# One transformer-like step on one core: slabs of gate_f on GpSimd's queue, an earlier split of a raw tile, and squares of the residual added by VectorE

## Chip, cores and metric

The kernel runs on one core of one Trainium2 chip. The metric is device time in microseconds (us) of one execution, as the median of the runs. Engines are named as in the profile: PE is TensorE (PEld its weight loads), DVE is VectorE, ACT is ScalarE, POOL is GpSimd, SP is SyncE. SP only issues DMAs here; ACT and POOL issue some too. L309 and the like are line numbers of the kernel before.

## What is computed

One layer over 128 context tokens and 256 latent tokens, 384 in all, with a model width of 2048. The part that the change touches is the second half, the MLP:

```python
def _layer(x, mod, ...):
    shift_a, scale_a, gate_a, shift_f, scale_f, gate_f = [mod[:, i][:, None, :] for i in range(N_MOD)]
    ...
    x = x + gate_a * _rmsnorm(mix, norm_w[1])
    h = _rmsnorm(x, norm_w[2]) * (1 + scale_f) + shift_f
    y = jnp.square(jax.nn.relu(h @ w1)) @ w2          # w1: 2048 x 8192, w2: 8192 x 2048
    x = x + gate_f * _rmsnorm(y, norm_w[3])
    return x, C, n, m
```

`mod` is `silu(cond) @ ada_w + ada_b` with ada_w of 2048 x 12288; the condition is one vector for the context tokens and one for the latent tokens. Everything is float32.

## The kernel before

**Products in three parts.** A float32 product is made of three faster ones: each operand is split into `hi` (a copy rounded to fp32r, made by ACT, L138 or L1223) and `lo = raw - hi` (made by DVE, L139 or L1224), and TensorE adds hi*hi, hi*lo and lo*hi (mm3, or `product` in mlp_seven). Every weight tile is 128 x 1024 floats and thus costs one load, one ACT pass and one DVE pass. Four `hi` and four `lo` buffers stand between the splitting engines and TensorE (N_W), so both can run about four tiles ahead.

**The order of work.** In the MLP a planner lays out each engine's instructions: it takes them in the order in which the code asks for them, but an instruction that is ready by its own reckoning may go ahead of one asked for earlier that is not. Once laid out, each engine and each DMA queue runs strictly in order. A `Feed` steps a side generator along a main loop: `first_side` is stepped once after each weight tile of the first w1 groups.

**The stage of the first w1 groups (some 615 to 670 us).** `make_h2` turns each of 16 tiles of the residual into the hi and lo parts of the MLP's input h2, with five DVE passes and two ACT passes that matter (L1025 to L1033). `gemm_T` over the first three w1 groups asks for h2 tiles 0 to 3 with its first weight tile, 4 to 7 with its fourth, 8 to 11 with its seventh and 12 to 15 with its tenth. Beside it `first_side` asks for the squares of the same 16 tiles: ACT squares a tile (L1046), and POOL (tiles 1 to 11) or DVE (tiles 12 to 15) adds it into `sqb` (L1047). The sum goes through TensorE (L925) to the factor `r2bc`, which the evaluation of the w1 groups needs.

**Chunks 1 to 6 of the MLP (some 810 to 1560 us).** A chunk is eight tiles of the hidden width. For each there are four groups of w1 (`w1_group`, four weight tiles each) and two blocks of w2 (`mlp_seven`, one for each half of the output). A block works on a 2 x 2 scheme with seven products: raw tiles b11, b21, b22 and b12 are loaded (L1218) and split, then differences of raw tiles are made by DVE in place (L1271, L1280, L1288, L1300) and split too, 14 splits in all. A chunk 7 with one such block closes the MLP.

**gate_f.** The last of the six modulation vectors is made on the side, by DVE: `ada_vec` loads a slab of ada_w (L309), multiplies it by the condition and adds it into an accumulator (L324, L326), once for each of the two conditions. Its first parts run in the earlier stages. Its last two parts run in chunks 1 to 4: 16 slabs of 128 x 512 floats each, through one buffer (`slab=512, bufs=1`, L1347), so that a slab's load waits for the DVE steps on the slab before it. Their loads stand on SP's queue among the loads of w1 (L132) and w2 (L1218). POOL's queue has the stores of x1 (L1055) until 740 us and the loads of x1 and gate_f for the end of the kernel from 1552 us on (L1149, L1155).

Of the kernel before, what the change touches and what calls it, by code (L numbers as in the profile page):

```python
# [10 lines left out]
ALU = mybir.AluOpType  # L11
# [5 lines left out]
NTOK = 384  # L17
# [11 lines left out]
N_ADA = 4  # L29
# [15 lines left out]
def hymba_kernel(  # L45
# [6 lines left out]
    nc = tc.nc  # L52
# [6 lines left out]
    adap = ada_scope.enter_context(tc.tile_pool(name="adap", bufs=1, side="right"))  # L59
# [239 lines left out]
    vec = {}  # L299

    def ada_vec(i, c, n):


        acc = vec["acc"].tile([P, 2, n], F32, tag="adaacc", name=f"ada_acc_{i}_{c}", bufs=1)
        c0, nj = i * D + c, vec["slab"] // n

        def load(t):
            raw = vec["pool"].tile([P, nj, n], F32, tag="ada", name=f"ada_raw_{i}_{c}_{t}", bufs=vec["bufs"])
            nc.sync.dma_start(raw, aw[:, nj * t:nj * t + nj, c0:c0 + n])  # L309
            return raw  # L310

        beside = vec.get("beside", {})
        raw = load(0)
        yield
        for t in range(16 // nj):
            if t in beside:
                next(beside[t], None)
            more = t < 16 // nj - 1
            ahead = load(t + 1) if more and vec["bufs"] > 1 else None
            for a in range(nj):  # L320
                for g in range(2):
                    cj = sg[:, g, nj * t + a:nj * t + a + 1]
                    if t == 0 and a == 0:
                        nc.vector.tensor_scalar(acc[:, g, :], raw[:, a, :], cj, None, op0=ALU.mult)  # L324
                    else:
                        nc.vector.scalar_tensor_tensor(acc[:, g, :], raw[:, a, :], cj, acc[:, g, :], op0=ALU.mult, op1=ALU.add)  # L326
            raw = load(t + 1) if more and ahead is None else ahead
            if more:
                yield
        yield  # L330
        w = n // 2
        nk = w // P
        if "end" in beside:
            next(beside["end"], None)
        ps = bank(f"adav_{i}_{c}")
        for h in range(2):
            for g in range(2):
                r = 32 * (2 * h + g)
                nc.tensor.matmul(ps[r:r + 32, 0:w], ones[:, 0:32], acc[:, g, h * w:(h + 1) * w], start=True, stop=True)
        sb = vec["pool"].tile([P, 512], F32, tag="adasb", name=f"adav_sb_{i}_{c}", bufs=1)  # L340
        nc.scalar.activation(sb[:, 0:w], ps[:, 0:w], AF.Copy)
        yield
        pf = bank(f"adaf_{i}_{c}")
        for k in range(nk):
            nc.tensor.matmul(pf[:, 4 * k:4 + 4 * k], sb[:, k * P:(k + 1) * P], ident[:, 0:P:32], start=True, stop=True)
        for h in range(2):
            ada_finish(i, c // P + nk * h, nk, pf[:, 0:4 * nk].rearrange("p (k r) -> p k r", r=4)[:, :, 2 * h:2 * h + 2])
        yield
# [87 lines left out]
    h = []  # L436
# [389 lines left out]
    att_scope = ExitStack()  # L826
    acc_scope = ExitStack()
    accp = acc_scope.enter_context(tc.tile_pool(name="accp", bufs=1, side="right", reuse_waits="tile"))
    vec.update(pool=adap, acc=accp, slab=1024, bufs=N_ADA)
    att = att_scope.enter_context(tc.tile_pool(name="att", bufs=2, reuse_waits="tile"))  # L830

    gslab = att.tile([P, 1, 512], F32, name="gslab", bufs=1)
# [205 lines left out]
            make_h2(len(h2))  # L1038
        return h2[k]

    def square_x1(k, eng):
        if k == 0:
            nc.scalar.activation(sqb[:, 0:NTOK], mo[k][:, 0:NTOK], AF.Square)
            return
        t = slot(f"sq_x1{k}")
        nc.scalar.activation(t[:, 0:NTOK], mo[k][:, 0:NTOK], AF.Square)  # L1046
        eng.tensor_tensor(sqb[:, 0:NTOK], sqb[:, 0:NTOK], t[:, 0:NTOK], op=ALU.add)  # L1047

    def store_x1():
        for k in range(KT):  # L1050
# [59 lines left out]
    late = []  # L1110

    def first_side():
        for n in range(3):
            if n == 0:
                with tc.issue_after(mm3.ins):
                    next(gfg)
            yield
            for k in range(4 * n, 4 * n + 4):
                square_x1(k, nc.gpsimd)
            yield  # L1120
            yield
        for k in range(12, 16):
            square_x1(k, nc.vector)
        yield
        late.append(nc.vector.tensor_copy(r2bc, token_rstd_rows([sqb], "r2")[:, 0:NTOK]).ins)
        yield
        yield
        yield from store_x1()
# [80 lines left out]
    def mlp_seven(ch, q, r16, r7):  # L1209
# [50 lines left out]
        for h in range(2):  # L1260
            b11, b21 = raws[0, 0, h], raws[1, 0, h]
            w = split(b21, f"b21{h}")
            product("yz0", 1, 0, h, w)
            product("2", 1, 1, h, w)
            if h == 0:
                w = split(raws[0, 0, 1], "b111")
                for js in ((0,), (1,)):
                    product("x", 0, 0, 1, w, js=js)
                    product("1", 0, 1, 1, w, js=js)
            b22, b12 = raws[1, 1, h], raws[0, 1, h]  # L1270
            tt(b11, b12, b11, op=ALU.subtract)  # L1271
            w = split(b22, f"b22{h}")
            product("yz1", 1, 0, h, w, stop=False)
            product("3", 2, 2, h, w)
            if h == 0:
                yx = ys[0].rearrange("p (a q) -> p a q", a=2)
                tt(yx, banks["x"].unsqueeze(1).to_broadcast([P, 2, 512]), yx, op=ALU.add)
            else:
                add(ys[0][:, 0:512], "yz0")
            tt(b12, b22, b12, op=ALU.subtract)  # L1280
            w = split(b11, f"t1{h}")
            product("yz1", 0, 0, h, w, start=False)
            product("4", 2, 0, h, w)
            if h == 0:
                keep(r16[:, q, 0], "1")
            else:
                add(ys[1][:, 0:512], "2")
            tt(b22, b22, b11, op=ALU.subtract)  # L1288
            free.append(b11)
            if h == 0:  # L1290
                load(1, 1, 1)
            w = split(b12, f"t3{h}")
            product("7", 0, 2, h, w)
            free.append(b12)
            if h == 0:
                load(0, 1, 1)
            else:
                add(ys[1][:, 512:], "3")
                add(ys[0][:, 512:], "yz1")
            tt(b21, b21, b22, op=ALU.subtract)  # L1300
            w = split(b22, f"t2{h}")
            product("6", 2, 1, h, w)
            free.append(b22)
            if h == 1:
                add(ys[2][:, 512:], "4")
                keep(r7[:, q], "7")
            w = split(b21, f"t4{h}")
            product("5", 1, 2, h, w)
            free.append(b21)
# [21 lines left out]
    for ch in range(8):  # L1331
# [6 lines left out]
        elif ch <= S_LAST:  # L1338
            if ch == S_FIRST:
# [4 lines left out]
                    scope.close()  # L1344
                str_scope = ExitStack()
                strp = str_scope.enter_context(tc.tile_pool(name="strp", bufs=1, side="right", reuse_waits="tile"))
                vec.update(pool=strp, acc=strp, slab=512, bufs=1, half=False)  # L1347
                ff.rate = RATE_GS
                r16, r7 = strp.tile([P, 2, 2, 512], F32, name="r16"), strp.tile([P, 2, 512], F32, name="r7")
                for n in range(3):  # L1350
# [80 lines left out]
```

## Time and profile before

| | us |
|---|---|
| median of 3 runs | 1679.78 |
| lowest and highest | 1679.76, 1680.25 |
| the profiled execution | 1679.09 |
| its span (first instruction to last) | 1677.4 |
| granted TensorE clock, mean | 0.998 |

In the views of the profile, "a <- b" in a list of waits means that a waited for b; a row of the timeline has its start from the span's beginning, its length, engine, line, operation, output and inputs, and in brackets the idle time of the engine before it. A run of equal instructions on one engine is one row with its count, and its length is that of the whole run. Where an engine has work all the time but shares of it wait for nothing, its speed alone counts: TensorE is in that state for nearly the whole MLP, so that a wait of another engine matters only where it makes TensorE wait.

### The profile page before, as it was taken

What the parts mean: (1) busy time and instruction counts of PE and PEld (TensorE: products, weight loads), DVE (VectorE), ACT (ScalarE), POOL (GpSimd) and SP (SyncE); (2) the same over time, 40 slices, a digit from 0 to 9 for tenths busy, and PEclk for the clock granted to TensorE, in tenths of its full rate; (3) what the DMA queues carried; (4) which work ended last, traced back from release to release, by engine and by line L of the source; (5) the groups of instructions that cost most, each with busy time, mean ns of one, the idle gap of its engine ahead of it and who ended that gap; (6) DMA issues with size and microseconds to landing.
All of it is one profiled execution on the core that took longest, in us unless ns stands there. A gap on an engine that the chain in (4) does not pass through costs nothing.

```text
span 1677.4 us, 24412 instructions
## 1 busy us (share of the span) xinstructions
PE 1648.3 (98%) x9249; PEld 1496.6 (89%) x9249; DVE 1328.4 (79%) x1971; ACT 751.1 (45%) x1224; POOL 133.1 (8%) x185
## 2 busy tenths in 40 slices
PE   6999999999999999999999999999999999999997
PEld 4888999999999989989988988988988988988986
DVE  3677669898999959997688787589788488488687
ACT  5322345555443345543444444444445354354452
POOL 1000002221000024530000000000000000000220
PEclk9999999999999999999999999999999999999999
DMA  9999757787789964754446445255544343443662
GB/s 328 329 309 304 246 175 247 239 250 229 239 262 309 319 202 137 213 153 126 136 150 203 125 133 177 87 169 162 153 151 136 116 151 116 136 125 112 197 193 103
DMA packets 231461, 320.72 MB, mean 191 GB/s; under 512 B 14784, under 2 KB 169872, under 8 KB 230960
## 3 DMA queue, kind: packets, MB, share of 16 engines
q1 hardware_dynamic: 223920, 303.42, 57.3%
q0 software_dynamic: 5984, 13.78, 2.9%
q10 hardware_dynamic: 1440, 1.97, 0.3%
q8 instruction: 72, 1.18, 0.3%
q14 instruction: 45, 0.37, 0.1%
HBM read 308.61 MB, written 10.51 MB: 190 GB/s over the span
## 4 chain that ended last, share of the span: by engine, by line
PE 78%; DVE 13%; DMA 5%; issue 3%; ACT 0%; POOL 0%; SPq 0%; DVEq 0%; ACTq 0%; POOLq 0%
PE acc_w L151 10%; PE acc_w L150 10%; PE acc_w L149 10%; PE v L512 4%; PE u L512 4%; PE y L1239 3%; PE y L1240 3%; PE y L1238 3%; DVE ada_acc L326 3%; DMA ada_raw<-in_ada_w_dram 2%; DVE lo_t L1224 2%; PE y L1082 2%; PE y L1083 2%; PE y L1081 2%; PE y_yz L1240 1%
## 5 line engine op out<-in xcount | busy, mean ns | idle before, releaser
L150 PE MATMUL acc_w<-h2l,hi_w 128*128 128x384 f32 (+1 forms) x1024 | 346.0, 338 | 0.5 <-DVE h2l L1033 0.5
L149 PE MATMUL acc_w<-h2h,hi_w 128*128 128x384 f32 (+1 forms) x1024 | 344.7, 338 | 1.2 <-ACT h2h L1029 1.2
L151 PE MATMUL acc_w<-h2h,lo_w 128*128 128x384 f32 (+1 forms) x1024 | 344.9, 337 | 0.6 <-DVE lo_w L139 0.6
L326 DVE SCALAR_TENSOR_TENSOR ada_acc<-ada_raw,sg,ada_acc 128x1024 f32<-128x1024 f32 (+1 forms) x240 | 252.8, 1081 | 32.1 <-DMA ada_raw<-in_ada_w_dram 32.1
L149 PEld LDWEIGHTS acc_w<-h2h,hi_w 128*128 128x128 f32 x1024 | 192.2, 188 | 4.0 <-ACT h2h L1029 2.0
L150 PEld LDWEIGHTS acc_w<-h2l,hi_w 128*128 128x128 f32 x1024 | 192.5, 188 | 1.8 <-DVE h2l L1033 0.8
L151 PEld LDWEIGHTS acc_w<-h2h,lo_w 128*128 128x128 f32 x1024 | 192.1, 188 | 2.2 <-DVE lo_w L139 1.9
L139 DVE TENSOR_TENSOR lo_w<-raw_b,hi_w 128x1024 fp32r<-128x1024 f32 x52 | 62.9, 1219 | 37.5 <-ACT hi_w L138 37.5
L139 DVE TENSOR_TENSOR lo_w<-raw_a,hi_w 128x1024 fp32r<-128x1024 f32 x52 | 63.1, 1219 | 35.7 <-ACT hi_w L138 35.6
L138 ACT ACTIVATE hi_w<-raw_b 128x1024 fp32r<-128x1024 f32 x52 | 54.9, 1057 | 62.7 <-PE acc_w L150 47.6
L138 ACT ACTIVATE hi_w<-raw_w 128x1024 fp32r<-128x1024 f32 x48 | 50.7, 1055 | 68.7 <-PE acc_w L150 36.5
L1223 ACT ACTIVATE hi_t<-raw_b 128x1024 fp32r<-128x1024 f32 x52 | 55.2, 1062 | 58.5 <-PE y L1240 28.3
L1223 ACT ACTIVATE hi_t<-raw_a 128x1024 fp32r<-128x1024 f32 x52 | 55.2, 1061 | 54.3 <-PE y L1240 26.5
L138 ACT ACTIVATE hi_w<-raw_a 128x1024 fp32r<-128x1024 f32 x52 | 54.8, 1057 | 53.6 <-PE acc_w L150 41.0
L139 DVE TENSOR_TENSOR lo_w<-raw_w,hi_w 128x1024 fp32r<-128x1024 f32 x48 | 58.4, 1218 | 22.0 <-ACT hi_w L138 21.9
L138 ACT ACTIVATE hi_wo<-raw_wo 128x1024 fp32r<-128x1024 f32 x32 | 33.9, 1063 | 80.1 <-DMA raw_wo<-in_w_out_dram 65.1
L1224 DVE TENSOR_TENSOR lo_b<-raw_b,hi_b 128x1024 fp32r<-128x1024 f32 x40 | 48.8, 1221 | 24.9 <-ACT hi_b L1223 24.6
L1223 ACT ACTIVATE hi_b<-raw_a 128x1024 fp32r<-128x1024 f32 x38 | 40.2, 1058 | 62.2 <-PE acc_w L150 46.2
L1223 ACT ACTIVATE hi_b<-raw_b 128x1024 fp32r<-128x1024 f32 x40 | 42.3, 1057 | 56.6 <-PE acc_w L150 45.3
L1224 DVE TENSOR_TENSOR lo_b<-raw_a,hi_b 128x1024 fp32r<-128x1024 f32 x38 | 46.2, 1221 | 22.4 <-ACT hi_b L1223 22.4
L1224 DVE TENSOR_TENSOR lo_t<-raw_a,hi_t 128x1024 fp32r<-128x1024 f32 x52 | 63.0, 1214 | 0.3 <-ACT hi_t L1223 0.2
L1224 DVE TENSOR_TENSOR lo_t<-raw_b,hi_t 128x1024 fp32r<-128x1024 f32 x52 | 62.9, 1215 | 0.0
(2286 smaller groups left out, 4243.7 us busy)
## 6 DMA issues: line engine op xcount, KB each, us to landing
ada_raw<-in_ada_w_dram SPq DMA_DIRECT2D x130, 512.0 KB, 5.2
raw_a<-in_w_dram SPq DMA_DIRECT2D x104, 512.0 KB, 4.1
raw_b<-in_w_dram SPq DMA_DIRECT2D x104, 512.0 KB, 4.2
raw_w<-in_w_dram SPq DMA_DIRECT2D x48, 512.0 KB, 4.2
raw_wo<-in_w_out_dram SPq DMA_DIRECT2D x32, 512.0 KB, 5.3
u<-in_ada_w_dram SPq DMA_DIRECT2D x18, 512.0 KB, 5.9
raw_u<-in_w_in_dram SPq DMA_DIRECT2D x16, 512.0 KB, 7.0
raw_q<-in_w_in_dram SPq DMA_DIRECT2D x16, 512.0 KB, 5.0
```

The source lines that it names most:

```text
L138: nc.scalar.activation(hi[:, 0:n], raw[:, 0:n], AF.Copy)
L139: low = lambda: nc.vector.tensor_tensor(lo[:, 0:n], raw[:, 0:n], hi[:, 0:n].bitcast(F32), op=ALU.subtract)
L149: nc.tensor.matmul(ps, lh, rh, start=start, stop=False)
L150: nc.tensor.matmul(ps, lh, rl, start=False, stop=False)
L151: mm3.ins = nc.tensor.matmul(ps, ll, rh, start=False, stop=stop).ins
L326: nc.vector.scalar_tensor_tensor(acc[:, g, :], raw[:, a, :], cj, acc[:, g, :], op0=ALU.mult, op1=ALU.add)
L512: nc.tensor.matmul(acc[i][:, 0:n], h[k0 + k][a][:, i * P:(i + 1) * P], (hi, lo)[b][:, k, :], start=k == 0 and a + b == 0, stop=k == nk - 1 ...
L1223: nc.scalar.activation(hi, raw, AF.Copy)
L1224: nc.vector.tensor_tensor(lo, raw, hi.bitcast(F32), op=ALU.subtract)
L1238: nc.tensor.matmul(banks[m], xh, wh, start=start and h + j == 0, stop=False)
L1239: nc.tensor.matmul(banks[m], xh, wl, start=False, stop=False)
L1240: nc.tensor.matmul(banks[m], xl, wh, start=False, stop=stop and h + j == 2)
```

## The change

Three edits that have nothing to do with each other.

1. The queue of `ada_vec`'s loads is given by its caller: SP's for the parts before chunk 1, POOL's for the last two parts of gate_f (32 slabs of 256 KB).
2. In a block of mlp_seven the split of b22 is asked for before, not after, the difference `b12 - b11`. Both were there before; neither reads what the other writes.
3. All adds of the squares are on DVE. `first_side` asks for squares 0 to 3 in its fourth step (before: second), 4 to 7 in its seventh (before: fifth), 8 to 15 in its tenth (before: 8 to 11 in the eighth, 12 to 15 in the tenth). The step that makes r2bc is the eleventh, as before.

```diff
@@ ada_vec
-            nc.sync.dma_start(raw, aw[:, nj * t:nj * t + nj, c0:c0 + n])
+            vec["queue"].dma_start(raw, aw[:, nj * t:nj * t + nj, c0:c0 + n])
...
-    vec.update(pool=adap, acc=accp, slab=1024, bufs=N_ADA)
+    vec.update(pool=adap, acc=accp, slab=1024, bufs=N_ADA, queue=nc.sync)
...
-    def square_x1(k, eng):
+    def square_x1(k):
...
-        eng.tensor_tensor(sqb[:, 0:NTOK], sqb[:, 0:NTOK], t[:, 0:NTOK], op=ALU.add)
+        nc.vector.tensor_tensor(sqb[:, 0:NTOK], sqb[:, 0:NTOK], t[:, 0:NTOK], op=ALU.add)
...
     def first_side():
+        with tc.issue_after(mm3.ins):
+            next(gfg)
         for n in range(3):
-            if n == 0:
-                with tc.issue_after(mm3.ins):
-                    next(gfg)
-            yield
-            for k in range(4 * n, 4 * n + 4):
-                square_x1(k, nc.gpsimd)
             yield
             yield
-        for k in range(12, 16):
-            square_x1(k, nc.vector)
+            yield
+            for k in range(4 * n, 4 * n + 4 if n < 2 else 16):
+                square_x1(k)
         yield
...
@@ mlp_seven
             b22, b12 = raws[1, 1, h], raws[0, 1, h]
+            w = split(b22, f"b22{h}")
             tt(b11, b12, b11, op=ALU.subtract)
-            w = split(b22, f"b22{h}")
             product("yz1", 1, 0, h, w, stop=False)
...
-                vec.update(pool=strp, acc=strp, slab=512, bufs=1, half=False)
+                vec.update(pool=strp, acc=strp, slab=512, bufs=1, half=False, queue=nc.gpsimd)
```

## What I predicted

> **What bounds the kernel now.** I read the page's busy times and its chain first, then TensorE's waits, then the table of windows, and only then the lines that the change touches.
>
> ```profile
> PE 1648.3 (98%) x9249; PEld 1496.6 (89%) x9249; DVE 1328.4 (79%) x1971; ACT 751.1 (45%) x1224; POOL 133.1 (8%) x185
> PE 78%; DVE 13%; DMA 5%; issue 3%; ACT 0%; POOL 0%; SPq 0%; DVEq 0%; ACTq 0%; POOLq 0%
> ```
>
> TensorE is busy for 98% of the span and holds 78% of the chain. All three edits act on other engines, so they can move the end only where TensorE waits for those. The waits of TensorE by releaser, first from 618 to 640 us (the first w1 groups, where the squares lie), then from 640 us to the end (total, times, longest):
>
> ```profile
> PE acc_w L149 <- ACT h2h L1029: 0.6, 1, 0.6
> PE acc_w L150 <- DVE h2l L1033: 0.5, 1, 0.5
> ...
> PE y L1238 <- ACT hi_t L1223: 1.4, 1, 1.4
> PE acc_w L151 <- DVE lo_w L139: 0.6, 2, 0.3
> PE y L1239 <- DVE lo_t L1224: 0.3, 1, 0.3
> PE y L1082 <- DVE lo_w L139: 0.2, 1, 0.2
> PE y_yz L1239 <- DVE lo_b L1224: 0.2, 1, 0.2
> ```
>
> That is 1.1 us and 2.7 us. What all three edits can save while TensorE has work is thus some 4 us, or 0.23% of the run. What they can cost has no such cap.
>
> Does time that TensorE gains at 636 us reach the end? It does if VectorE waits for TensorE further on. The table of windows (length, then busy time of PE, PEld, DVE, ACT, POOL; granted clock; DMA share; GB/s):
>
> ```profile
> 780.00:820.00 40.00, 40.00 (x236) 39.34 (x235) 19.76 (x31) 16.03 (x25) 0.00 (x0) 1.00 0.49 151
> 908.00:945.00 37.00, 37.00 (x213) 37.00 (x212) 23.21 (x35) 14.12 (x22) 0.00 (x0) 1.00 0.66 198
> 945.00:987.00 42.00, 42.00 (x199) 36.16 (x198) 39.58 (x47) 21.92 (x27) 0.00 (x0) 1.00 0.41 122
> 1208.00:1247.00 39.00, 39.00 (x182) 33.27 (x181) 37.75 (x45) 20.20 (x24) 0.00 (x0) 1.00 0.40 116
> ```
>
> From 780 to 820 us VectorE is busy for 19.76 of 40 us beside a full TensorE: it follows TensorE, and an earlier TensorE carries it along. The second row is a stretch of w1 groups: 213 matmuls in 37.0 us, 0.174 us each. In the blocks of mlp_seven (the last two rows) it is nearly full, 39.58 of 42 us and 37.75 of 39 us. There its lead is spent, and there the waits of 2.7 us lie.
>
> **The squares (square_x1, first_side).** Removed from GpSimd are 11 adds, added to VectorE are 11. GpSimd's adds together (min/median/max in ns), the last of the four that VectorE has already, GpSimd's first three, VectorE's and ScalarE's rows beside them, and TensorE's two waits:
>
> ```profile
> L1047 POOL TENSOR_TENSOR sqb<-sqb,sq_x x11: 1003/1222/3058, 624.0 to 652.8; 128x384 f32<-128x384 f32 x11
> 661.96 0.55 DVE L1047 TENSOR_TENSOR sqb<-sqb,sq_x 128x384 f32<-128x384 f32 x1
> 623.98 3.41 POOL L1047 TENSOR_TENSOR sqb<-sqb,sq_x 128x384 f32<-128x384 f32 x3 [11.14 <-ACT sq_x L1046]
> 601.28 0.24 DVE L297 TENSOR_TENSOR mod<-mod,prmT 128x8 f32<-128x8 f32 x2
> 624.53 0.69 DVE L297 TENSOR_TENSOR mod<-mod,prmT 128x4 f32<-128x4 f32 x1
> 625.40 0.91 DVE L297 TENSOR_TENSOR mod<-mod,prmT 128x4 f32<-128x4 f32 x1
> 626.62 1.31 DVE L1030 SCALAR_TENSOR_TENSOR h2l<-mo,mod,h2h 128x128 fp32r<-128x128 f32 x2
> 634.40 0.74 DVE L1030 SCALAR_TENSOR_TENSOR h2l<-mo,mod,h2h 128x128 fp32r<-128x128 f32 x2
> 634.08 1.75 ACT L1046 ACTIVATE sq_x<-mo 128x384 f32<-128x384 f32 x4
> 635.74 0.19 ACT L1032 ACTIVATE h2h<-mod 128x2 fp32r<-128x2 f32 x1
> 633.24 0.34 PE L151 MATMUL acc_w<-h2h,lo_w 128*128 128x386 f32 x1
> 634.23 0.80 PE L149 MATMUL acc_w<-h2h,hi_w 128*128 128x386 f32 x3 [0.65 <-ACT h2h L1029]
> 635.22 0.34 PE L149 MATMUL acc_w<-h2h,hi_w 128*128 128x386 f32 x1
> 636.08 0.44 PE L150 MATMUL acc_w<-h2l,hi_w 128*128 128x386 f32 x1 [0.53 <-DVE h2l L1033]
> ```
>
> A pair of L297 takes 0.24 us where GpSimd is still. Inside GpSimd's stretch (623.98 to 627.39) single ones take 0.69 and 0.91 us and end with GpSimd's add; of the pair of L1030 at 626.62, 0.57 us is the same (1.31 against 0.74). Taking 0.16 us for a lone L297 (an estimate: 0.24 less a step of about 0.08), VectorE loses 0.53 + 0.75 + 0.57 = 1.85 us before it makes h2 of tile 7, for which TensorE waits from 633.4 to 634.2: 0.99 us between starts where matmuls stand 0.17 us apart, a stall of 0.8 us. The second, 0.86 - 0.17 = 0.7 us, comes of ScalarE: four squares of 1.75 us stand ahead of the L1032 at 635.74 that L1033 reads. The new code asks for those squares two steps later (call 7 in place of call 5 of the generator) and for squares 0 to 3 at call 4 in place of 2, behind the h2 tiles that this group needs.
>
> Added before 636 us on VectorE are at most the three adds of squares 1 to 3: 3 x 0.55 = 1.65 us, less than the 1.85 us that go. If they come early, the first stall stays almost whole and the second goes: 0.7 + 0.2 = 0.9 us. If they come late, both go: 1.5 us. I take 1.3 us, nearer to the second, since they are asked for later. Over the whole stage the 11 adds cost VectorE 11 x 0.55 = 6 us at most; what is later stretched beside GpSimd's other eight adds pays for part of it. What could be late next is the sum of squares:
>
> ```profile
> 665.93 0.72 PE L925 MATMUL tr_r<-cst,sqb 128*128 128x1 f32 x6
> ```
>
> The last add (661.96) ends at 662.51 and TensorE, in order, takes it up at 665.93: 3.4 us in hand, 2.1 us when TensorE is 1.3 us earlier. So no loss is booked; the cover is gone if the last add slips by over 2 us.
>
> **The fourth raw tile split ahead of the weight sum (mlp_seven).** Nothing is added or removed; lo of b22 and the sum of L1271 change places in the order of asking. VectorE's order here is laid out by the planner by what is ready, and hardly ever are both ready at once. Where they are, late in a block:
>
> ```profile
> 1149.59 1.22 DVE L1271 TENSOR_TENSOR raw_b<-raw_a,raw_b 128x1024 f32<-128x1024 f32 x1
> 1150.73 1.22 DVE L1224 TENSOR_TENSOR lo_b<-raw_b,hi_b 128x1024 fp32r<-128x1024 f32 x1
> ```
>
> the lo comes 1.14 us sooner and the sum, whose result ScalarE splits next, 1.14 us later. VectorE's total stays, so the stalls at a block's end stay. The bounds are 0.2 us gained (all of TensorE's wait at lo_b) and 1.1 us lost per place; I take zero.
>
> **The slabs on GpSimd's queue (ada_vec).** Moved are the 32 slabs of gate_f's last two parts, each into the one buffer, so that each load waits for VectorE's two steps on the last, and those wait for the landing. The slabs' issues (KB each, median us to landing), VectorE's waits for them (total, times) and their least, median and longest landing; then the nearest loads on GpSimd's queue in the same two views; then a load behind a slab, and VectorE beside it:
>
> ```profile
> ada_raw<-in_ada_w_dram SPq DMA_DIRECT2D x32, 256.0 KB, 2.8
> DVE ada_acc L326 <- DMA ada_raw<-in_ada_w_dram: 32.1, 19, 2.9
> DMA to landing us min/median/max: 2.6/2.8/6.9
> ...
> x1t<-x_dram POOLq DMA_DIRECT2D x15, 192.0 KB, 4.2
> DMA to landing us min/median/max: 3.2/4.1/4.6
> ...
> 918.86 0.37 SPq L1218 DMA_DIRECT2D raw_b<-in_w_dram  x1
> ...
> 917.62 1.22 DVE L139 TENSOR_TENSOR lo_w<-raw_b,hi_w 128x1024 fp32r<-128x1024 f32 x1
> 920.54 1.42 DVE L326 SCALAR_TENSOR_TENSOR ada_acc<-ada_raw,sg,ada_acc 128x512 f32<-128x512 f32 x2 [1.70 <-DMA ada_raw<-in_ada_w_dram]
> ```
>
> What SyncE's queue gains: the load behind a slab goes out at 918.86, which is when VectorE's lo_w of 917.62 has ended (918.84), so it waited for its own buffer and not for the slab. I found no load behind a slab whose own releaser was earlier than the slab. Unblocking is worth nothing here.
>
> What it costs: the loads of x1t, at most 192 KB, land after 3.2 to 4.6 us, the slabs on SyncE's after 2.8 us in the median. I take 3.8 us, so 1.0 us more a slab (bounds: 0.4 us by the fastest of x1t; below nothing for the few slabs that now land in up to 6.9 us behind weight loads). VectorE waits for a slab 19 times. Where TensorE has lead to spend, 1 us hides; and the planner lays VectorE's order anew, so that some steps will move behind another split. Between nothing and the slower rival's 15 us I take 0.5 us: half of one such wait, in a block without lead.
>
> The Trainium skill (page "DMA: Bandwidth & Descriptors", section "Specifications") speaks against this edit: it gives about 1 us to the first byte on GpSimd's path and about 0.6 us on SyncE's. By it the estimate would be 0.4 us more a slab in place of 1.0, and the rival's price under half; no run here shows the first byte itself.
>
> **The sum.** -1.3 + 0 + 0.5 = -0.8 us. The profiled execution took 1679.09 us, 0.7 us under the median of the runs (1679.78), so its own sum is 1678.3 us; against the median I forecast **1679.0 us**. About 0.2%, 3.4 us, is what a measurement of this kernel can tell from no change: "same" reaches from 1676.4 to 1683.1.
>
> **The rivals.**
>
> *Slower: the slab's cycle outruns TensorE's step.* VectorE's waits for slabs in two stretches of w1 groups, from 908 to 945 us and from 1166 to 1208 us:
>
> ```profile
> DVE ada_acc L326 <- DMA ada_raw<-in_ada_w_dram: 10.8, 7, 2.3
> DVE ada_acc L326 <- DMA ada_raw<-in_ada_w_dram: 11.8, 7, 2.9
> ```
>
> A split serves 24 matmuls here (4 tiles x 2 halves x 3 products), 24 x 0.174 = 4.2 us, and one slab cycle is also 4.2 us (2.8 us landing and 1.42 us of steps). At 3.8 us it is 5.2 us; if the order keeps one slab to a split, VectorE falls back by 1 us at each of the seven waits of a stretch. Of these 7 us it wins back its idle time in the block that follows, 42.0 - 39.58 = 2.4 and 39.0 - 37.75 = 1.2 us: 4.6 and 5.8 us late. The other 19 - 14 = 5 waits lie in or near blocks whose ends stall already: 5 us. In all 15 us, 1679.8 - 1.3 + 15 = 1693.5 us. It decides as soon as the slab lands over 2.8 us after its issue with the order kept. For it: 14 of 19 waits lie in those two stretches with the cycle at the step. Against it: the order is laid out anew. Chance 0.15. With only the 5 waits in blocks late, 1679.8 - 1.3 + 5 = 1683.5 us: another 0.15.
>
> *Faster: the stalls go as well.* A slower slab cycle pushes VectorE's steps out of the blocks into the w1 groups, and slabs no longer queue behind weight loads (the 6.9 us). All of 1.5 + 2.7 us goes: 1675.6 us. For it, the blocks with waits of TensorE are mostly those with slab steps; against it, every stall must go. Chance 0.2.
>
> *Nothing is done.* The planner puts the adds into the same gaps, the slabs hide and b22 keeps its place: 1679.8 us, inside the forecast's own case. Forecast and this together: 0.5.
>
> **How the numbers follow.** The forecast's own range is 1677.5 to 1682. To hold 8 in 10 it reaches to the faster rival and most of the way to the slower one: 1675.6 to 1690. Faster 0.2, same 0.5, slower 0.15 + 0.15 = 0.3.
>
> **What would show it.** Squares: no GpSimd add from 620 to 660 us, L297 back under 0.2 us, TensorE's two waits before 640 us gone, L925 without a wait. Slabs: landing on GpSimd's queue near 3.8 us; VectorE's wait for them above 32.1 us in total where the order was kept; TensorE's waits from 860 to 1250 us tell whether they cost. The split: lo_b ahead of L1271 only late in blocks. I am wrong if a slab on GpSimd's queue lands as fast as on SyncE's, if TensorE's stalls of 2.7 us go whole, or if r2bc becomes late.

## The result, and the profile after

| | median us | runs | from to |
|---|---|---|---|
| before | 1680.01 | 6 | 1677.92 to 1680.97 |
| after | 1694.09 | 6 | 1689.89 to 1698.64 |

The ratio is 1.0088 with a 95% interval from 1.0078 to 1.0098: the changed kernel is slower by 14.1 us. The forecast was 1679.0 us in a range that ended at 1690.0; the slower rival had said 1693.5 us. The profiled execution of after took 1694.44 us, of which 1692.7 are its span; before's took 1679.09 and 1677.4. In the changed kernel the lines of mlp_seven stand three lower (L1224 is L1221 now, L1238 is L1235, L1288 is L1285, L1300 is L1297), and L1271 is L1269.

The busy times of after, from its page:

```profile
PE 1654.9 (98%) x9249; PEld 1499.5 (89%) x9249; DVE 1328.7 (78%) x1982; ACT 751.2 (44%) x1224; POOL 135.8 (8%) x206
```

VectorE has no more work: it is busy for 1328.7 us against 1328.4. TensorE issues the same 9249 matmuls but is busy for 6.6 us longer (1654.9 against 1648.3), to which I come below; the rest must be in waits. TensorE's waits in after, first from 600 to 640 us, then from 640 us to the end (total, times, longest):

```profile
PE acc_w L149 <- ACT h2h L1029: 0.5, 1, 0.5
PE tr_r L214 <- DVE dg_r L212: 0.2, 1, 0.2
...
PE y_x L1235 <- ACT hid38h L199: 5.3, 1, 5.3
PE y_x L1235 <- ACT hid14h L199: 2.2, 1, 2.2
PE y_yz L1236 <- DVE lo_b L1221: 1.9, 2, 1.3
```

The two waits that the prediction placed at 633 and 635 us are gone; what is left of the first stretch is 0.7 us, from before 618 us. Two new ones are large, and both are for a hid tile, which no row of before's waits names: hid14h and hid38h, the hi parts of two tiles of hidden units, which the products with the third weight tile of a block read. The slabs in after, from 800 to 1400 us: their issues (KB each, median us to landing), VectorE's waits for them, and their least, median and longest landing:

```profile
ada_raw<-in_ada_w_dram POOLq DMA_DIRECT2D x31, 256.0 KB, 3.1
DVE ada_acc L326 <- DMA ada_raw<-in_ada_w_dram: 52.1, 23, 4.6
DMA to landing us min/median/max: 2.7/3.1/6.0
```

They land after 3.1 us, not after the 3.8 us of the prediction, and VectorE still waits 52.1 us where it waited 32.1. One cycle shows why. VectorE's steps in the w1 groups before the second large stall (start, duration, in brackets the idle time before), then the loads between them on GpSimd:

```profile
1202.72 1.41 DVE L326 SCALAR_TENSOR_TENSOR ada_acc<-ada_raw,sg,ada_acc 128x512 f32<-128x512 f32 x2 [2.31 <-DMA ada_raw<-in_ada_w_dram]
1207.89 1.41 DVE L326 SCALAR_TENSOR_TENSOR ada_acc<-ada_raw,sg,ada_acc 128x512 f32<-128x512 f32 x2 [2.62 <-DMA ada_raw<-in_ada_w_dram]
1212.91 0.75 DVE L326 SCALAR_TENSOR_TENSOR ada_acc<-ada_raw,sg,ada_acc 128x512 f32<-128x512 f32 x1 [1.42 <-DMA ada_raw<-in_ada_w_dram]
```

```profile
1204.43 0.54 POOL L309 DMA_DIRECT2D ada_raw<-in_ada_w_dram  x1 [4.32 <-DVE ada_acc L326]
1209.60 0.54 POOL L309 DMA_DIRECT2D ada_raw<-in_ada_w_dram  x1 [4.63 <-DVE ada_acc L326]
```

VectorE's pair ends at 1202.72 + 1.41 = 1204.13 and the load starts at 1204.43, 0.30 us later. From one pair to the next it is 5.17 and 5.02 us, with landings here of 3.37 and 3.29 us; TensorE's step is 4.2 us. That is the rival's cycle. Over all slabs that VectorE waited for, the medians are 0.30 us from the step's end to the load and 3.05 us to landing in after, 0.03 and 2.75 us in before: 0.27 + 0.30 = 0.57 us more a slab.

Now the stall itself. VectorE in after, then the same instructions in before (L968 and L970 are short sums in `evac_pair`, which makes the hid tiles out of a w1 group's results; ScalarE copies hid38h out of what L970 writes):

```profile
1224.90 1.42 DVE L326 SCALAR_TENSOR_TENSOR ada_acc<-ada_raw,sg,ada_acc 128x512 f32<-128x512 f32 x2 [1.98 <-DMA ada_raw<-in_ada_w_dram]
1226.23 1.22 DVE L1221 TENSOR_TENSOR lo_b<-raw_a,hi_b 128x1024 fp32r<-128x1024 f32 x1
1229.67 0.75 DVE L326 SCALAR_TENSOR_TENSOR ada_acc<-ada_raw,sg,ada_acc 128x512 f32<-128x512 f32 x1 [2.23 <-DMA ada_raw<-in_ada_w_dram]
1230.34 0.28 DVE L968 TENSOR_TENSOR s<-z,z 128x128 f32<-128x128 f32 x1
...
1231.68 0.28 DVE L970 TENSOR_TENSOR z<-z 128x128 f32<-128x128 f32 x1
```

```profile
1213.86 0.74 DVE L326 SCALAR_TENSOR_TENSOR ada_acc<-ada_raw,sg,ada_acc 128x512 f32<-128x512 f32 x1
1214.52 1.21 DVE L1224 TENSOR_TENSOR lo_b<-raw_b,hi_b 128x1024 fp32r<-128x1024 f32 x1
1216.22 1.23 DVE L1224 TENSOR_TENSOR lo_b<-raw_a,hi_b 128x1024 fp32r<-128x1024 f32 x1 [0.49 <-ACT hi_b L1223]
...
1218.62 0.28 DVE L968 TENSOR_TENSOR s<-z,z 128x128 f32<-128x128 f32 x1
1219.96 0.29 DVE L970 TENSOR_TENSOR z<-z 128x128 f32<-128x128 f32 x1
```

What waits for that L970 in after, on ScalarE and on TensorE:

```profile
1232.00 0.52 ACT L199 ACTIVATE hid38h<-z 128x384 fp32r<-128x384 f32 x1 [7.85 <-DVE z L970]
```

```profile
1226.85 0.40 PE L1237 MATMUL y<-hi_b,hid36l 128*128 128x512 f32 x1
1232.57 0.80 PE L1235 MATMUL y_x<-hi_b,hid38h 128*128 128x512 f32 x1 [5.33 <-ACT hid38h L199]
```

In before the last slab step of the part lies ahead of the last two splits, and L970 comes as soon as they are done. In after two slab steps stand among those splits, each with a wait of 2 us, and L968 and L970, which wait for no slab at all, stand behind them on the in-order engine. ScalarE starts on hid38h 0.04 us after L970 ends (1231.96), and TensorE, whose matmuls here start 0.23 us apart, has 5.72 us between two starts. VectorE's order is thus not the same as before. Ahead of the L970 that makes hid14 stand 7 slab instructions in after and 5 in before, one pair more.

The stall itself is only a part of what is lost there. The windows 830 to 840 and 1230 to 1240 us (length, then busy time of PE, PEld, DVE, ACT, POOL; granted clock; DMA share; GB/s) of before, then of after:

```profile
830.00:840.00 10.00, 10.00 (x45) 8.10 (x44) 9.14 (x12) 5.75 (x8) 0.00 (x0) 1.00 0.54 166
1230.00:1240.00 10.00, 10.00 (x45) 8.14 (x44) 10.00 (x12) 5.02 (x6) 0.00 (x0) 1.00 0.42 121
```

```profile
830.00:840.00 10.00, 7.45 (x26) 5.34 (x25) 10.00 (x15) 5.00 (x7) 0.00 (x0) 0.83 0.22 62
1230.00:1240.00 10.00, 7.40 (x18) 5.39 (x19) 10.00 (x15) 3.46 (x5) 0.00 (x0) 0.66 0.18 53
```

Right behind each of the two stalls TensorE's granted clock is at half for a while: the matmuls start 0.43 us apart (1235.27 and 1235.70 us, for one) in place of 0.23, and full speed is back at 836.4 and 1239.1 us. That costs up to 10 x (1 - 0.83) = 1.7 us and 10 x (1 - 0.66) = 3.4 us, together 5.1 us, and is most of TensorE's 6.6 us of longer busy time. At the second stall it makes (5.72 - 0.23) + 3.4 = 8.9 us lost, not 5.5. The clock in before stays at full speed from 600 us up to its last 7 us. The length of one wait doesn't tell whether a slow stretch follows: before's wait of 1.4 us near 1160 us has none behind it, the waits of 1.3 and 0.5 us for hid14h and hid14l in e1_slabs (a run of the next section) have one. Nor is the clock the whole loss: the run of after whose granted clock was 0.998, as in before, took 1689.89 us, 9.9 us over before.

### The profile page after: what moved, and what is told of

It reads as the page before. It is cut to its first block, busy times and chain, and to the rows that moved or that the text cites. A ratio compares the mean times of both kernels' runs of the same rounds, so it can differ in the third digit from the quotient of the medians.

```text
span 1692.7 us, 24418 instructions
## 1 busy us (share of the span) xinstructions
PE 1654.9 (98%) x9249; PEld 1499.5 (89%) x9249; DVE 1328.7 (78%) x1982; ACT 751.2 (44%) x1224; POOL 135.8 (8%) x206
## 5 line engine op out<-in xcount | busy, mean ns | idle before, releaser
L326 DVE SCALAR_TENSOR_TENSOR ada_acc<-ada_raw,sg,ada_acc 128x1024 f32<-128x1024 f32 (+1 forms) x240 | 252.3, 1080 | 52.2 <-DMA ada_raw<-in_ada_w_dram 52.1
L1221 DVE TENSOR_TENSOR lo_b<-raw_b,hi_b 128x1024 fp32r<-128x1024 f32 x40 | 48.7, 1221 | 24.0 <-ACT hi_b L1220 23.9
L1221 DVE TENSOR_TENSOR lo_t<-raw_a,hi_t 128x1024 fp32r<-128x1024 f32 x52 | 63.2, 1215 | 1.6 <-ACT hi_t L1220 1.3
L1221 DVE TENSOR_TENSOR lo_t<-raw_b,hi_t 128x1024 fp32r<-128x1024 f32 x52 | 62.9, 1215 | 0.0
L1221 DVE TENSOR_TENSOR lo_b<-raw_a,hi_b 128x1024 fp32r<-128x1024 f32 x38 | 46.2, 1221 | 18.7 <-ACT hi_b L1220 18.7
```

What stands on the lines that cost most here:

```text
L1221: nc.vector.tensor_tensor(lo, raw, hi.bitcast(F32), op=ALU.subtract)
```

## The experiments

Each run was timed against the kernel before on the same chip. Ratios are to that, with the 95% interval; its median was 1679.77 us beside e1 to e4, 1680.64 beside e5 to e8 and 1679.67 beside the rest. The ratios are those on record and are not exactly quotients of these medians.

| run | what it is | median us | ratio |
|---|---|---|---|
| e1_slabs | slabs alone | 1693.48 | 1.0085 (1.0071 to 1.0098) |
| e2_squares | squares alone | 1679.76 | 0.9999 (0.9990 to 1.0008) |
| e3_split | split alone | 1680.52 | 1.0002 (0.9993 to 1.0010) |
| e4_no_slabs | squares and split | 1679.66 | 1.0004 (0.9995 to 1.0013) |
| e5_two_pool | after, two slab buffers, shared tile | 1686.47 | 1.0038 (1.0025 to 1.0052) |
| e6_two_sp | the same on SyncE's queue | 1680.35 | 1.0001 (0.9992 to 1.0009) |
| e7_pool_old_order | slabs alone, old order | 1684.44 | 1.0028 (1.0018 to 1.0038) |
| e8_sp_new_order | old queue, new order | 1687.60 | 1.0048 (1.0035 to 1.0062) |
| e9_two_pool_late | after, two slab buffers | 1680.42 | 1.0008 (1.0000 to 1.0017) |
| e10_two_sp_late | the same on SyncE's queue | 1675.57 | 0.9975 (0.9965 to 0.9985) |
| e12_squares_spread | squares alone, spread | 1678.27 | 0.9993 (0.9984 to 1.0002) |
| e13_two_sp_spread | spread, two buffers, SyncE | 1675.37 | 0.9974 (0.9962 to 0.9985) |

To see where a difference arises, I took from the trace the start of every matmul and subtracted the start of the same matmul in before, each as the median of 8 us on either side of a time of before. The first column is that difference at 600 us, ahead of all that the change touches; the others are what came on top. A step between two columns is time lost (or won) there by TensorE:

```
us in before         600 |  645   680   800   870   930  1000  1100  1155  1200  1230  1300  1600
after               -0.3 | -1.7  -0.5  -0.4   4.1   5.2   5.4   5.5   7.3   5.3  14.2  15.6  15.7
e1_slabs             0.7 |  0.0   0.2   0.2   4.2   5.7   6.1   6.1   5.9   4.0  12.4  13.6  13.4
e2_squares          -0.4 | -1.7  -0.7  -0.6  -0.5  -0.6  -0.6  -0.5   0.8   0.8   0.9   1.2   1.2
e3_split             0.9 |  0.0   0.2   0.2   0.2   0.7   0.7   0.7   0.7   0.7   0.7   0.7   0.6
e4_no_slabs          0.9 | -1.7  -1.1  -1.0  -1.0  -1.2  -1.2  -1.1  -1.1  -1.3  -1.3  -1.0  -1.0
e5_two_pool          6.2 | -1.7  -0.7  -0.9   0.3   1.3   1.3   1.2  -0.1  -2.1   1.5   1.7   1.2
e6_two_sp            6.8 | -1.7  -1.1  -1.3  -1.2  -0.6  -0.6  -0.7  -2.0  -4.0  -4.0  -3.8  -4.2
e7_pool_old_order   -0.1 |  0.0   0.4   0.4   1.2   2.3   2.6   2.7   3.5   3.5   5.3   5.3   5.2
e8_sp_new_order      0.9 |  0.0   0.5   0.5   6.7   7.3   8.3   8.3   7.5   5.5   6.6   7.8   7.6
e9_two_pool_late    -0.3 | -1.7  -0.3  -0.2   2.5   2.3   2.4   2.4   1.3  -0.7   4.2   4.6   4.5
e10_two_sp_late     -0.5 | -1.7  -1.0  -0.9  -0.9  -1.3  -1.2  -1.2  -2.3  -4.3  -4.3  -3.9  -3.8
e12_squares_spread  -0.1 | -1.7  -0.5  -0.3  -0.3  -0.2  -0.3  -0.4  -0.5  -0.7  -0.7  -0.5  -0.7
e13_two_sp_spread   -1.0 | -1.7  -0.5  -0.4  -0.3  -0.7  -0.8  -0.9  -2.1  -4.1  -4.1  -3.9  -4.0
```

These are single executions: the first column alone moves by up to a microsecond either way, e5 and e6 apart. Some steps hold a stretch at half clock behind a stall, as in after: 1.7 us (3.4 us at half) from 800 to 870 us in after, e1_slabs and e8_sp_new_order, 3.4 us (6.8 us at half) from 1200 to 1230 us in after and e1_slabs, and 1.7 us near 1225 to 1233 us in e5_two_pool and e9_two_pool_late. The other runs have none from 600 to 1660 us.

### One part at a time

e1_slabs has only the queue of the slabs, e2_squares only the squares, e3_split only the split, and e4_no_slabs is after with one word put back:

```diff
-                vec.update(pool=strp, acc=strp, slab=512, bufs=1, half=False, queue=nc.gpsimd)
+                vec.update(pool=strp, acc=strp, slab=512, bufs=1, half=False, queue=nc.sync)
```

> Only the slabs on GpSimd's queue. Theory (the slab's cycle outruns TensorE's step, all by itself): a landing of 3.1 us against 2.8 us and a start of the load some 0.3 us later, in an order of VectorE's work that keeps a slab to nearly every split; 12 to 17 us slower than the kernel before (1692 to 1697 us), with TensorE waiting over 1 us in two or three places between 820 and 1250 us. Rival 1 (the three edits together laid VectorE's order anew, and that order costs): within 4 us of the kernel before. Rival 2 (the loss is of the slabs, but the other edits made half of it): 5 to 9 us slower.

> Only the squares of the residual on VectorE, asked for later. Theory: the two waits at 633 and 635 us go (1.5 us) and two small ones come at 659 and 670 us, where the sum of squares is now later: 0.4 to 1.0 us faster than the kernel before. Rival 1 (the prediction's term): 1.3 us faster, the sum in time. Rival 2 (VectorE's later order is changed by the edit): over 2 us slower.

> Only the fourth raw tile split ahead of the first weight sum. Theory (both are seldom ready at once): within 0.5 us of the kernel before, and TensorE's waits for lo_b between 0 and 1 us in total. Rival (the sum that comes 1.1 us later delays a split that TensorE waits for, in some of the 13 blocks): 2 to 8 us slower, with waits at the products of the summed tiles.

> The changed kernel with the slabs back on SyncE's queue (squares and split stay as changed). Theory (the slabs' queue alone makes the loss): 0.3 to 1.3 us faster than the kernel before, so 14 to 16 us faster than the changed kernel. Rival (order laid anew by the squares and the split): still 4 us or more slower than the kernel before.

The slabs alone cost 1.0085, 14.3 us by that ratio, all of the loss. The other two together leave the time where it was. So the cause is in one edit, and the rival that the three together made it has fallen. TensorE's waits of e1_slabs after 640 us:

```profile
PE y_x L1238 <- ACT hid38h L199: 5.7, 1, 5.7
PE y_yz L1239 <- DVE lo_b L1224: 1.6, 1, 1.6
PE y_x L1238 <- ACT hid14h L199: 1.3, 1, 1.3
```

These are the same two hid tiles. In the table above e1_slabs loses 4.0 us between 800 and 870 us and 8.4 us between 1200 and 1230 us; two places make 12.4 of 13.4 us, and of these 5.1 us are the half clock.

The squares alone were expected to bring 0.4 to 1.0 us and brought nothing that can be measured. TensorE does win 1.7 us by 645 us, but 1.0 of it is gone by 680 us, and 1.3 us more go near 1155 us, far behind the edit, where TensorE waits for a split that VectorE makes late (TensorE's waits of e2_squares after 640 us):

```profile
PE y L1236 <- DVE lo_t L1221: 1.5, 2, 1.2
```

In before this was 0.3 us, in one place. In e4_no_slabs, with the split moved too, this second loss doesn't arise, so it isn't a price of the squares as such.

The split is nothing, as expected. Of the 26 places where a sum of L1271 and the lo of b22 are made, VectorE's order has the lo first in one place in e3_split, in none in before and in none in after.

### Queue or order

The slabs' queue changed two things: how long a slab takes, and the order that the planner laid out for VectorE. To part them, two kernels hold TensorE, VectorE and ScalarE to an order read out of another build, by dependencies that carry order alone. They cover the stretch in which the two orders differ. No run holds the old order on the old queue, so what the holding itself costs, if anything, is not parted from the results:

```diff
+    for names in ORDER:
+        for a, b in zip(names, names[1:]):
+            tc.add_manual_dep(traced[b], a, info, reason="order")
```

e7_pool_old_order has the slabs on GpSimd's queue in the order of before; e8_sp_new_order has them on SyncE's queue in the order of e1_slabs.

> Slabs alone on GpSimd's queue, while TensorE, VectorE and ScalarE are held to the very order of the kernel before. Theory Q (the later landing and the later start of the load do it): 10 to 16 us slower than the kernel before. Theory O (the planner takes a slab on GpSimd's queue to land sooner and puts it a place earlier in VectorE's order; that order is what costs): within 4 us of the kernel before. Both needed: 4 to 9 us slower.

> Slabs on SyncE's queue, while TensorE, VectorE and ScalarE are held to the very order of the kernel that has them on GpSimd's queue. Theory Q: within 3 us of the kernel before, since each slab lands 0.3 us sooner and starts 0.3 us sooner. Theory O: 9 to 14 us slower than the kernel before, with TensorE waiting for hid38h again. Both needed: 3 to 8 us slower.

Neither theory stands alone. The queue in the old order costs 1.0028, 4.7 us; the new order on the old queue costs 1.0048, 8.1 us; both together 14.3 us. (By the medians it is 3.8, 7.0 and 13.7 us.) In e8_sp_new_order TensorE waits 3.6 us for hid14h, and not for hid38h, as theory O had it. VectorE's waits for slabs and TensorE's waits after 640 us in e7_pool_old_order:

```profile
DVE ada_acc L326 <- DMA ada_raw<-in_ada_w_dram: 40.6, 21, 3.4
...
PE y_yz L1239 <- DVE lo_b L1224: 1.3, 1, 1.3
```

With the order held, 8.5 us more waiting of VectorE comes out as small waits of TensorE in many places: the longest that before doesn't have is 1.3 us. None of them has a stretch at half clock behind it. The table by time says where the two factors meet. Between 1200 and 1230 us the queue alone loses 1.8 us and the order alone 1.1 us, but both 8.4 us, of which 3.4 us are the half clock that only both together set off. The remaining 5.0 us are still more than 1.8 + 1.1. With the order alone, VectorE waits 1.71 and 1.57 us for the two slabs among the last splits, with both 2.24 and 2.25 us; with the queue alone no slab step stands there. Between 800 and 870 us the queue alone loses 0.8 us, both 4.0 us, and the order alone 6.2 us, more than both (1.7 us of the last two each are the half clock). There the order alone is a case of its own. VectorE in e8_sp_new_order:

```profile
817.83 0.48 DVE L324 TENSOR_SCALAR ada_acc<-ada_raw,sg 128x512 f32<-128x512 f32 x1 [6.38 <-DMA ada_raw<-in_ada_w_dram]
```

Its load on SyncE's queue with the one ahead, and the first of VectorE's steps on slabs in after (count, durations, first and last start):

```profile
810.94 0.47 SPq L1218 DMA_DIRECT2D raw_b<-in_w_dram  x1
811.46 0.47 SPq L309 DMA_DIRECT2D ada_raw<-in_ada_w_dram  x1
```

```profile
L324 DVE TENSOR_SCALAR ada_acc<-ada_raw,sg x4: 478/478/486, 809.2 to 1085.4; 128x512 f32<-128x512 f32 x4
```

On SyncE's queue the part's first slab goes out at 811.46 us, right behind a weight load, and VectorE gets it at 817.8; in after it goes out on GpSimd's queue at 777.1 us already, and VectorE is at work on it at 809.2. The new order counts on that. So 8.1 us isn't what the order costs on GpSimd's queue, and that 4.7 and 8.1 add up to nearly 14.3 is partly chance. What stands: the edit's loss needs the new order for 14.3 - 4.7 = 9.6 us of it, and the slower slab alone gives 4.7 us. In the profiled executions the half clock is 5.1 us of e1_slabs' loss and nothing of e7_pool_old_order's. How much of it a run pays at the end is open: the four runs of e1_slabs don't follow their granted clock (1693.07 us at 0.995, 1693.71 us at 0.997).

That the planner takes a slab on the other queue to be ready sooner would explain why it put the steps earlier; the orders show that it did, not why.

### A second buffer

If the cycle of one buffer is the cause, a load that goes out while VectorE works on the slab before must take most of it away on either queue. The space for a second slab comes from the small tile of a part's sums, which is laid into the accumulator, and from a scratch tile further on:

```diff
-        sb = vec["pool"].tile([P, 512], F32, tag="adasb", name=f"adav_sb_{i}_{c}", bufs=1)
+        sb = acc[:, 0, :] if vec["slab"] == n else vec["pool"].tile([P, 512], F32, tag="adasb", name=f"adav_sb_{i}_{c}", bufs=1)
...
-        jk = vec["pool"].tile([P, 512], F32, tag="adasb", name=f"jky{i}_{a}")
+        jk = vec["pool"].tile([P, 1, 512], F32, tag="ada", name=f"jky{i}_{a}", bufs=2)[:, 0, :]
...
-                vec.update(pool=strp, acc=strp, slab=512, bufs=1, half=False, queue=nc.gpsimd)
+                vec.update(pool=strp, acc=strp, slab=512, bufs=2, half=False, queue=nc.gpsimd)
```

e6_two_sp has queue=nc.sync in the last line.

> The changed kernel with two buffers for the slabs on GpSimd's queue (the small tile of each part's sums now lies in the accumulator, so that the space suffices): the next slab is asked for while VectorE works on the last. Theory (a slab's cycle of landing and steps, one buffer, is what outran TensorE): VectorE's waits for slabs fall from 52 us to under 10 us, TensorE no longer waits for hid14h or hid38h, and the time is that of the kernel before within 3 us (1677 to 1682 us). Rival (loads on GpSimd's queue cost in themselves, by their issue or by contention, whenever they are asked for): 8 us or more slower than the kernel before.

> The same two buffers with the slabs on SyncE's queue. Theory: as fast as the kernel before or up to 3 us faster, since VectorE's 32 us of waiting for slabs go and with them part of TensorE's 2.7 us of waits after 640 us (1676.5 to 1680 us); within 1.5 us of the two buffers on GpSimd's queue. Rival (VectorE's order, laid anew, keeps the stalls): within 1 us of the kernel before, with TensorE's waits after 640 us above 2 us.

Both missed, and the first column of the table says why: TensorE is 6.2 and 6.8 us late already at 600 us. The condition (slab equals n) also holds for the parts of the first stage, n = 1024, and there, as the code reads, the next part can't use the accumulator while the sums lie in it. The next two kernels leave the first stage as it was; the condition is `vec["slab"] == 512`:

> As the two buffers on GpSimd's queue, but the accumulator takes over the small tile in the late stage alone: in the earlier runs with two buffers TensorE's starts were already 6 to 7 us late at 560 us, before any slab of the late stage. Theory (that early delay comes of the shared tile, and one buffer's cycle is what costs in the late stage): within 3 us of the kernel before. Rival (GpSimd's queue costs even with the slab asked for ahead): 5 us or more slower, as with the tile shared everywhere.

> Two buffers with the slabs on SyncE's queue, the accumulator shared in the late stage alone; squares and split as changed. Theory: the early 6 us go as well, so 3 to 7 us faster than the kernel before (1673 to 1677 us), TensorE's gain lying between 1110 and 1170 us. Rival (the early delay was a chance of the profiled execution): 1679 to 1681 us.

That takes the early delay away (-0.3 and -0.5 us at 600 us), and two buffers on GpSimd's queue give 1.0008, 1.3 us slower than before and 13 us faster than after, as the theory had it. On SyncE's queue they give 0.9975, 4.2 us faster than before. VectorE's waits for slabs and their landing (800 to 1400 us) in e9_two_pool_late, then in e10_two_sp_late with its longest wait of TensorE after 640 us:

```profile
DVE ada_acc L326 <- DMA ada_raw<-in_ada_w_dram: 13.8, 10, 2.6
DMA to landing us min/median/max: 2.9/3.6/5.4
```

```profile
DVE ada_acc L326 <- DMA ada_raw<-in_ada_w_dram: 7.3, 9, 2.0
DMA to landing us min/median/max: 2.6/3.3/6.7
...
PE y L1236 <- DVE lo_t L1221: 0.3, 1, 0.3
```

The slabs land later than with one buffer (3.6 against 3.1 us, 3.3 against 2.8 us), and it matters little, since VectorE waits far less for them. The table puts most of the win of e10_two_sp_late between 1000 and 1200 us, 3.1 us. The second buffer is not the reason for all of it: 2.0 us are won between 1155 and 1200 us, where TensorE in before has its longest wait (1.4 us for hi_t, L1238), and after, e1_slabs and e8_sp_new_order win the same 2 us there with one buffer, while e7_pool_old_order wins nothing. So these 2 us go with VectorE's new order. Another 1.0 us is there by 680 us already, with the squares. No run has two buffers alone. The rest of the loss on GpSimd's queue lies where it lay, between 1200 and 1230 us (4.9 us in the profiled execution, which at a span of 1681.6 us is one of the longer runs; 1.7 us of it are the half clock), with hid38h again:

```profile
PE y_x L1235 <- ACT hid38h L199: 2.1, 1, 2.1
PE y_x L1235 <- ACT hid14h L199: 0.8, 1, 0.8
```

### The squares in fours

The eight adds at the end of the change's order seemed to make the sum of squares late. Here the twelve later squares are asked for in fours, too:

```diff
-        for n in range(3):
-            yield
-            yield
-            yield
-            for k in range(4 * n, 4 * n + 4 if n < 2 else 16):
-                square_x1(k)
+        n = 0
+        for at in (3, 2, 2, 2):
+            for _ in range(at):
+                yield
+            for k in range(n, n + 4):
+                square_x1(k)
+            n += 4
```

> The kernel before with the squares on VectorE, the first four asked for later as in the change, but the other twelve in fours at steps 5, 7 and 9 of the generator instead of four at step 6 and eight at step 9. Theory (in the change the eight adds at the end make the sum of squares late and give back 1.05 of the 1.7 us that TensorE gains at 633 to 636 us): TensorE's gain of 1.5 us or more is still there at 680 us; what reaches the end also hangs on VectorE's order after 1100 us, where the change's squares gave 1.3 us back: 0 to 2 us faster in all. Rival (VectorE has no room for twelve more adds there, wherever they are): 1 us is given back by 680 us again.

> Two buffers in the late stage with the slabs on SyncE's queue, the squares spread as in the run beside it, the split as in the kernel before. Theory: the gains add, 4 to 8 us faster than the kernel before (1672 to 1676 us). Rival (both remove the same waits, or VectorE's new order gives one of them back): 2 us or less faster than the kernel before, or no faster than two buffers with the change's squares.

My theory of the give-back fell. The last add starts at 664.10 us in place of 666.54, yet of 1.7 us won by 645 us 1.2 are gone by 680 us, as the rival said. The wait for h2l is there too, only at another time (the row of e12_squares_spread, then two of after):

```profile
656.23 0.45 PE L150 MATMUL acc_w<-h2l,hi_w 128*128 128x386 f32 x1 [0.29 <-DVE h2l L1030]
```

```profile
659.75 0.44 PE L150 MATMUL acc_w<-h2l,hi_w 128*128 128x386 f32 x1 [0.21 <-DVE h2l L1030]
670.77 0.59 PE L214 MATMUL tr_r<-dg_r,cst 128*128 128x384 f32 x1 [0.31 <-DVE dg_r L212]
```

In both placements something that TensorE needs comes late from VectorE, which is busy for 29 of 32 us there in before and in after (the windows in the last section). Whether another placement would do is open. The run as a whole is at 0.9993, not told apart from before. With two buffers on SyncE's queue the spread squares, without the move of the split, give 0.9974, no better than e10_two_sp_late with 0.9975: the gains do not add. Both are faster than the kernel before and than the changed one, and they are the fastest of all tried.

## Why the prediction was wrong

**The step that failed** is the term of the slabs, "Between nothing and the slower rival's 15 us I take 0.5 us: half of one such wait, in a block without lead". Measured alone, the slabs cost 14.3 us. I had both ends of the bound right and chose the wrong one, for two reasons, both written down there. I let "the planner lays VectorE's order anew" count as relief and as evidence against the rival. Two thirds of the loss need the new order: e7_pool_old_order, with the order held, loses 4.7 us. And I counted on TensorE's lead, without looking at which instructions of VectorE have none.

**The rival's price was right in part by luck, its places were wrong.** It had 4.6 and 5.8 us in the two stretches of w1 groups and 5 us in blocks. In e1_slabs the first stretch costs TensorE 0.4 us (930 to 1000 us in the table); VectorE's waits there are covered. The losses lie in two blocks, 4.0 and 8.4 us, and 5.1 of these 12.4 us are TensorE at half clock behind its stalls, a cost that neither the forecast nor the rival has. What the second stretch took from VectorE came out all at once, at the first matmul that reads hid38. I had priced late lo splits and overlooked L968 and L970, the short sums of evac_pair, behind which ScalarE and TensorE stand.

**The landing was off in the other direction.** I took 3.8 us, from x1t's loads; it was 3.05 us in the median, 0.30 us above SyncE's. The 0.27 us by which the load starts later after VectorE's step was not in the prediction. Together 0.57 us, a little over half of the 1.0 us taken: even so it was enough, since the cycle had been at TensorE's step already. The figures that the prediction quotes from the Trainium skill (page "DMA: Bandwidth & Descriptors", section "Specifications") differ by 0.4 us between the two paths; the 0.30 us in landing agree with that in sign and nearly in size, and the later start comes on top.

**"Unblocking is worth nothing here"** is not contradicted by any run for SyncE's weight loads. It missed the slab's side: the first slab of the first of the two parts no longer stands behind weight loads, and the new order makes use of it (809.2 us against 817.8 us in e8_sp_new_order).

**The squares, -1.3 us.** The mechanism was right: no add on GpSimd, L297 short, both waits gone, 1.7 us won against 0.9 to 1.5 predicted. What failed is "no loss is booked" for what is late next. The cover was said to be gone if the last add slips by over 2 us; it slipped from 662.51 to 667.09 us, 4.6 us. But the slip is not shown to be the cause: in e12_squares_spread the last add starts 2.4 us sooner than in after, and as much is given back. By 680 us 0.7 us is left of the gain in the run with the squares alone, and nothing measurable at the end.

**The split, 0.** Right: alone it changes one place of 26, in after none, and the time doesn't change.

## What to carry to other kernels

Where one buffer is loaded, used and loaded again beside a step of about the same length, the cycle of landing, use and the way back to the queue is a clock of its own: 0.57 us more on it cost 4.7 us here with the order held, and 14.3 us with the order that the planner made of it. A change of queue also changes what a planner believes to be ready, so compare the order of the in-order engines before and after, and look for what waits for nothing itself but stands behind the slow step. When TensorE has stalled, look at its granted clock behind the stall too, since the waits alone don't add up to the loss. The remedy was no queue but a second buffer: it took 13 of the 14 us back on the slow queue. On the fast one the kernel was 4.2 us faster than the old one, together with the moved squares and VectorE's new order.

## What the runs showed of the hardware

Behind some stalls of TensorE its granted clock was 0.5 for 3.4 us (e8_sp_new_order, e9_two_pool_late, the first stall of after) or 6.8 us (the second stall of after), and its matmuls of 128x512 then started 0.43 us apart in place of 0.23.

A load on GpSimd's queue starts 0.30 us after the step of VectorE that it waits for has ended, and its issue takes 0.54 us; on SyncE's queue it is 0.03 and 0.34 us. This is the same in all kernels with one buffer (0.295 to 0.299 us over some 30 slabs each, against 0.027 to 0.028). The issue of one and the same load, in after and in before:

```profile
L309 POOL DMA_DIRECT2D ada_raw<-in_ada_w_dram x31: 536/538/543, 811.0 to 1226.6; - x31
```

```profile
L309 SPq DMA_DIRECT2D ada_raw<-in_ada_w_dram x32: 327/341/498, 810.0 to 1207.8; - x32
```

The eleven adds of 0.55 us that VectorE took over cost it nothing in busy time. The windows 600 to 640 and 640 to 672 us (length, then busy time of PE, PEld, DVE, ACT, POOL; clock; DMA share; GB/s) of before, then of after:

```profile
600.00:640.00 40.00, 38.15 (x264) 34.65 (x263) 29.25 (x73) 20.33 (x48) 10.18 (x10) 1.00 0.45 145
640.00:672.00 32.00, 32.00 (x183) 31.73 (x182) 29.07 (x59) 16.33 (x32) 13.66 (x15) 1.00 0.48 147
```

```profile
600.00:640.00 40.00, 39.32 (x273) 36.44 (x273) 28.77 (x80) 20.16 (x47) 0.88 (x1) 1.00 0.46 150
640.00:672.00 32.00, 31.48 (x176) 30.24 (x176) 29.31 (x61) 17.16 (x34) 5.61 (x8) 1.00 0.44 130
```

VectorE is busy for 58.3 us in before and 58.1 us in after, and over the whole run for 1328.4 us in before and 1328.1 us in e2_squares, with eleven instructions more: what its own instructions had been stretched by beside GpSimd's adds is about as much as the adds themselves. The two L297 that took 0.69 and 0.91 us take 0.16 and 0.15 us now (620 to 640 us, durations in ns):

```profile
L297 DVE TENSOR_TENSOR mod<-mod,prmT x2: 152/156/161, 624.2 to 624.6; 128x4 f32<-128x4 f32 x2
```

The Trainium skill (page "SBUF — State Buffer", section "Who interferes with whom") says that VectorE and GpSimd share a pair of ports under an exclusive lock; these rows agree with it.
